# Float32 values in the first head group's attention, values' products set together, and squared blocks added before their product with ones

## The chip, the cores and the metric

The kernel runs on one core of a Trainium2 chip. The metric is the device time of one execution in microseconds (us); the runs shown of the kernel before took 2036.65, 2031.55 and 2031.51 us, with a median of 2031.55. The five engines are called TensorE (PE, with its weight loads as PEld), VectorE (DVE), ScalarE (ACT), GpSimd (POOL) and SyncE (SP).

## The reference

A bidirectional encoder of two layers on x of 1024 tokens by 1024, float32. Each layer mixes three groups of channels and then has a gated feed-forward part:

```python
h = _rmsnorm(x, g_pre_mix[l])
zf, zq, zk, zv, zm = jnp.split(h @ w_in[l], splits, axis=-1)     # 256, 512, 128, 128, 256
y_f = _fourier_mix(zf, w_fourier[l])
y_a = _window_attn(rope(q), rope(k), v, sink[l])    # 8 query heads, 2 key/value heads of 64
y_m = _memory_attn(zm, km, vm)                      # 4 heads over 256 memory rows
y = jnp.concatenate([_rmsnorm(y_f, ..), _rmsnorm(y_a, ..), _rmsnorm(y_m, ..)], -1) @ w_out[l]
x = x + _rmsnorm(y, g_post_mix[l])
gate, up = jnp.split(_rmsnorm(x, g_pre_ffn[l]) @ w_ffn_in[l], 2, axis=-1)
x = x + _rmsnorm((silu(gate) * up) @ w_ffn_out[l], g_post_ffn[l])
```

In the window attention a block of 128 queries sees its own block of keys and the one on each side (two at the ends). Query heads 0 to 3 share key/value head 0, and heads 4 to 7 share head 1; in the kernel these are head groups g = 0 and g = 1. The norms of y_f, y_a and y_m need the mean of squares of each token over its group's channels.

## The kernel before, in words

**Tiles.** Tokens are cut into NT = 8 tiles of 128. Most large products are made from numbers split into a high part, rounded to a format of TensorE (float32r), and the low rest: `split` (L174) copies the high part on ScalarE (L176) and subtracts on VectorE or POOL (L177). Such a product is three matmuls of high and low parts (`Acc`, L179). Some products are plain float32 matmuls, which the chip runs as two passes, so that the trace has two records for each.

**Stages of a layer.** Projections of keys, values and memory queries (`kvz`, L714), woven with the Fourier group; projections of queries (`q`, L761), woven with attention over memory (`mem_units`, L935); window attention of head group 0, woven with the output products of the Fourier and memory groups (`fm_units`, L1006) and the loads of w_out; window attention of group 1, woven with the output product of the attention group, the residual and the norm (`out`, L1061) and the first blocks of the feed-forward part (`Blocks`, L1081; `Quad`, L1135); then the feed-forward part, which the change does not edit.

**Window attention.** `att_scores` (L777) makes the scores of 4 heads, the exponentials (ScalarE, L801) and scales them by the reciprocal sums (POOL, L812). One tile later `att_values` (L817) transposes the probabilities of each key block j on TensorE into a PSUM tile `pT` (L825, four transposes), copies that to SBUF and multiplies it with the values. For group 0 the copy is a split (ScalarE L176, VectorE L177), and each of the two parts is the moving side (512 columns) of one matmul whose stationary side holds the high and the low values side by side (L840, tile `av`, 128 columns). `fold` (L855) then adds the two halves of the result: two copies on ScalarE (L861) and two additions on VectorE (L863). For group 1 `values_32` (L846) has first added high and low values into float32; the copy of `pT` is one ScalarE copy (L830) that separates heads by parity, and two float32 matmuls with 64 stationary columns, one for each half s of the array, multiply it (L833), just behind the copy of each block j.

**Attention over memory.** `mem_values` (L928) makes, for two heads, four float32 matmuls of 64 stationary and 512 moving columns (L932, tile `mav`): two memory blocks mt by two halves s.

**Sums of squares.** `group_scale` (L980) squares a tile on ScalarE (L985) into w blocks of 128 by 128, and adds over channels with w matmuls, each with a block as the stationary side and a 128x2 tile of ones as the moving side (L988, tile `ssp`). w is 2 for the memory group's tiles (from `fm_units`) and 4 for the attention tiles (from `out_prep`, L1050). The mean (L990, VectorE) and the power -1/2 (L992, POOL) give the scale by which the output product is later taken out of PSUM (L1031, L1072).

**Order.** The code issues work in units that `weave` and the loop at L1443 interleave; a scheduler in the framework then sets the order of each engine's instructions, and every engine works its own list in that order. Operands wait for each other by semaphores. Memory is laid out by hand: `at` gives places in a float32r and a float32 area in steps of 256 columns, and the places listed in `TURNED` are pieces of their own that `turned` and `reflex` turn from one type to the other; a piece is only turned when all that use it are done.

## Time and profile before

| what | value |
|---|---|
| three runs, us | 2036.65, 2031.55, 2031.51 (median 2031.55) |
| the profiled execution, us | 2032.38 |
| its span, first to last instruction, us | 2030.4 |
| granted TensorE clock over the span | 0.994 |
| instructions | 28325 |
| HBM | 220.11 MB read, 66.58 MB written, 141 GB/s |
| layer 0: group 0's wide value products | 223.1 to 281.5 us |
| layer 0: group 1's value products | 293.8 to 370.7 us |
| layer 1: the same two | 1218.6 to 1280.3 and 1288.7 to 1369.1 us |

The profile is one execution on the chip. Each engine's busy time is the union of its instructions; the chain of work that ended last follows, from the last instruction back, what released each step. Groups collect the instructions of a line. The matmuls of TensorE overlap in the pipeline, so the time that one holds the engine is read from its start to the next one's start and not from its own length.

### The profile page before, as it was taken

How to read it: one execution, taken by the hardware profiler on the slowest of the kernel's cores; microseconds unless marked ns; L12 is line 12 of the kernel's file. 1: busy time of each engine (PE TensorE's matmuls, PEld its weight loads, DVE VectorE, ACT ScalarE, POOL GpSimd, SP SyncE). 2: the span in 40 equal slices, each digit the busy share in tenths (PEclk: the TensorE clock that was granted, in tenths of full speed). 3: DMA queues.
4: the chain of work that ended last, by engine and by line, in shares of the span. 5: the costliest groups of instructions: out<-in, count | busy, mean ns of one | idle time of the engine just before them, and what ended most of it. 6: DMA issues, size and time to landing. Idle time of an engine off the chain costs nothing.

```text
span 2030.4 us, 28325 instructions
## 1 busy us (share of the span) xinstructions
PE 1984.7 (98%) x9587; PEld 1631.2 (80%) x9587; DVE 1492.6 (74%) x2346; ACT 1049.7 (52%) x2204; POOL 684.9 (34%) x811
## 2 busy tenths in 40 slices
PE   8999999999999999999999999999999999999998
PEld 7877878778888888887888778877788888887886
DVE  5566767897877776778876668679786776778766
ACT  6476877643333333554555768686333333346441
POOL 4344445224334333002423644451433433410011
PEclk9999999999999999999999999999999999999999
DMA  6110333434333324879831113244333323269973
GB/s 213 62 58 22 109 104 115 146 109 130 104 109 100 103 88 139 297 266 324 286 142 54 54 58 115 85 144 135 106 118 114 116 82 114 96 209 354 314 265 125
DMA packets 181889, 288.56 MB, mean 142 GB/s; under 512 B 15560, under 2 KB 81648, under 8 KB 181744
## 3 DMA queue, kind: packets, MB, share of 16 engines
q1 hardware_dynamic: 173680, 267.88, 39.7%
q10 hardware_dynamic: 8064, 18.88, 2.4%
q8 instruction: 75, 1.23, 0.2%
q14 instruction: 70, 0.57, 0.1%
HBM read 220.11 MB, written 66.58 MB: 141 GB/s over the span
## 4 chain that ended last, share of the span: by engine, by line
PE 86%; DVE 5%; DMA 3%; ACT 2%; issue 2%; POOL 1%; SPq 0%; DVEq 0%; POOLq 0%; ACTq 0%
PE fo L1330 17%; PE qc L1181 11%; PE qx L1181 11%; PE qy L1181 11%; PE mo L187 8%; PE qz L1181 5%; PE kvp L187 4%; PE qp L187 3%; PE zT L187 2%; PE sc L788 2%; PE pT L825 2%; PE av L833 1%; PE qa L1181 1%; PE mav L932 1%; PE av L840 1%
## 5 line engine op out<-in xcount | busy, mean ns | idle before, releaser
L1330 PE MATMUL fo<-arena_r 128*128 128x512 f32 x1512 | 354.2, 391 | 6.0 <-ACT big L1355 3.8
L1330 PEld LDWEIGHTS fo<-arena_r 128*128 128x128 f32 x1512 | 283.6, 188 | 65.6 <-ACT big L1355 4.6
L176 ACT CAST arena_r<-arena_f 128x512 fp32r<-128x512 f32 (+2 forms) x344 | 185.9, 571 | 179.5 <-DMA arena_f<-actd 66.6
L1181 PE MATMUL qc<-arena_r,flex 128*128 128x512 f32 x912 | 220.2, 390 | 0.0
L177 DVE TENSOR_TENSOR arena_r<-arena_f,arena_r 128x512 fp32r<-128x512 f32 x262 | 182.0, 727 | 46.9 <-ACT arena_r L176 39.0
L1171 ACT CAST flex<-arena_f 128x512 fp32r<-128x512 f32 x148 | 91.9, 621 | 235.0 <-PE qy L1181 73.3
L1181 PEld LDWEIGHTS qc<-arena_r,flex 128*128 128x128 f32 x912 | 171.2, 188 | 37.0
L1181 PE MATMUL qy<-arena_r,flex 128*128 128x512 f32 x576 | 139.9, 390 | 2.3 <-ACT flex L1171 2.3
L1171 ACT CAST arena_r<-arena_f 128x512 fp32r<-128x512 f32 x92 | 57.1, 621 | 159.1 <-DVE arena_f L1168 63.6
L1172 DVE TENSOR_TENSOR flex<-arena_f,flex 128x512 fp32r<-128x512 f32 x148 | 110.9, 750 | 28.4 <-ACT flex L1171 28.2
L1181 PEld LDWEIGHTS qy<-arena_r,flex 128*128 128x128 f32 x576 | 107.9, 188 | 25.3 <-ACT flex L1171 2.7
L1215 POOL TENSOR_TENSOR arena_f<-arena_f 128x512 f32<-128x512 f32 x36 | 47.3, 1315 | 237.5 <-ACT arena_f L1186 237.5
L1181 PE MATMUL qx<-arena_r 128*128 128x512 f32 x360 | 119.5, 389 | 0.0
L1181 PE MATMUL qy<-arena_r 128*128 128x512 f32 x480 | 116.7, 390 | 0.0
L1172 DVE TENSOR_TENSOR arena_r<-arena_f,arena_r 128x512 fp32r<-128x512 f32 x92 | 68.2, 742 | 63.2 <-ACT arena_r L1171 62.8
L1181 PE MATMUL qz<-arena_r,flex 128*128 128x512 f32 x320 | 106.8, 395 | 0.0
L1181 PEld LDWEIGHTS qy<-arena_r 128*128 128x128 f32 x480 | 90.3, 188 | 18.9 <-ACT arena_r L1171 0.2
L1168 DVE TENSOR_TENSOR arena_f<-arena_f 128x512 f32<-128x512 f32 x90 | 98.1, 1098 | 5.5 <-DMA arena_f<-in_w_ffn_in 3.9
L1222 POOL TENSOR_TENSOR arena_f<-arena_f 128x512 f32<-128x512 f32 x36 | 60.0, 1667 | 120.2 <-DVE arena_f L1221 120.2
L187 PE MATMUL mo<-big,arena_r 128*128 128x512 f32 x384 | 100.2, 399 | 0.3 <-ACT arena_f L1031 0.2
L1181 PE MATMUL qx<-flex,flex 128*128 128x512 f32 x304 | 100.1, 390 | 0.0
L1242 POOL TENSOR_TENSOR arena_f<-arena_f,flex 128x512 f32<-128x512 f32 x32 | 51.8, 1619 | 139.5 <-ACT flex L1233 83.7
(315 smaller groups left out, 4659.8 us busy)
## 6 DMA issues: line engine op xcount, KB each, us to landing
arena_f<-in_w_ffn_out SPq DMA_DIRECT2D x264, 256.0 KB, 4.7
actd<-arena_f SPq DMA_DIRECT2D x154, 256.0 KB, 2.5
arena_f<-actd SPq DMA_DIRECT2D x154, 256.0 KB, 4.4
arena_f<-in_w_ffn_in SPq DMA_DIRECT2D x46, 512.0 KB, 3.7
big<-in_w_ffn_in SPq DMA_DIRECT2D x40, 512.0 KB, 4.5
arena_f<-in_w_in SPq DMA_DIRECT2D x40, 256.0 KB, 2.9
arena_f<-in_x SPq DMA_DIRECT2D x16, 512.0 KB, 4.3
arena_f<-in_w_out SPq DMA_DIRECT2D x32, 256.0 KB, 2.7
```

The costliest lines, as they stand in the source:

```text
L176: nc.scalar.copy(hi, src)
L177: return (lo_eng or nc.vector).tensor_tensor(out=lo, in0=src, in1=f32(hi), op=ALU.subtract)
L187: mm(self.dst, a, b, start=self.i == 0, stop=self.i == self.n - 1)
L788: mm(pt, lhs, self.kst[g][i][:, k0 * P : k1 * P], start=i == 0, stop=i == 1)
L1168: nc.vector.tensor_tensor(out=s, in0=x, in1=y, op=op)
L1171: self.cast = nc.scalar.copy(w[:, 0], s)
L1172: nc.vector.tensor_tensor(out=w[:, 1], in0=s, in1=f32(w[:, 0]), op=ALU.subtract)
L1181: mm(pt, a, b, start=start and n == 0, stop=n == 11, skip_group_check=not start)
L1215: G(out=self.u2, in0=self.u2, in1=self.p1, op=ALU.add)
L1222: G(out=self.p5, in0=self.p1, in1=self.p5, op=ALU.add)
L1242: (G if i % 2 else V).tensor_tensor(out=a[i], in0=c, in1=g[i], op=ALU.mult)
L1330: mm(pt, ab[:, 0, x, sl], ab[:, 1, y], start=new and first and j == 0, stop=last and j == 2, skip_group_check=not new)
```

## The change

Three edits, and what goes with them:

- **Group 0 as group 1.** The values of both groups are kept in float32 (`v32`, one POOL copy for each tile in `kvz`), and group 0 takes the same path as group 1: one copy of `pT`, two 64-column float32 matmuls for each block, one eviction. In group 0 the copies of `pT` alternate between VectorE and ScalarE; in group 1 all are on ScalarE. The split of the values, `values_32` and `fold` are gone. There are 8 places for the copies in place of 4.
- **Products together.** In `att_values` the matmuls of a tile are issued after all its transposes and copies, with the last block first; in `mem_values` the four are issued with the second block and the second half first.
- **Squares added.** `group_scale` adds the squared blocks on VectorE by halving (4 to 2 to 1, or 2 to 1), so that one product with ones is left. Attention tiles 6 and 7 keep their four products.

Places 16 and 96 become pieces that can be turned; they are turned back to float32r in the pass i == NT of the loop, before the blocks of the feed-forward part that lie there.

```diff
-TURNED = {32: 8, 56: 8, 112: 8, 120: 4}
+TURNED = {16: 8, 32: 8, 56: 8, 96: 8, 112: 8, 120: 4}
...
+    def together(products):
+
+        for i, p_ in enumerate(products):
+            p_(i < 2, i >= len(products) - 2)
...
                 if half == 0:
+                    self.v32 = turned(96, 2, 2, NT, HD)[:, 0]
...
-            vst = self.vst[half][:, c]
-            split(vst[:, :, 0, :], vst[:, :, 1, :], r[:, P : 2 * P].rearrange("p (g d) -> p g d", g=2), nc.gpsimd)
+            nc.gpsimd.tensor_copy(self.v32[:, :, t, :], r[:, P : 2 * P].rearrange("p (g d) -> p g d", g=2))
...
             av = ps([512], "av", "av")
+            pfs = []
             for j in range(nk):
                 pT = ps([4, P], "pT", "pT")
                 for h in range(4):
                     nc.tensor.transpose(pT[:, h, :], es_[h // 2][:, h % 2, j * P : j * P + P], ident)
-                if g:
-
-                    pf = self.pfs[self.pfi % 4]
-                    self.pfi += 1
-                    nc.scalar.copy(pf, pT.rearrange("p (k s) q -> p s k q", s=2))
-                    for s in range(2):
-                        rhs = pf[:, s].rearrange("p k q -> p (k q)")
-                        mm(av[64 * s : 64 * s + 64, 0 : 2 * P], self.v32[:, k0 + j], rhs, start=j == 0, stop=j == nk - 1)
-                    continue
-                pp = phs(2, 512, dt=F32R)
-                ph, pl = pp[:, 0], pp[:, 1]
-                split(ph, pl, pT.rearrange("p h q -> p (h q)"))
-                lhs = self.vst[(k0 + j) // 4][:, (k0 + j) % 4, g].rearrange("p a d -> p (a d)")
-                for i, p_ in enumerate((ph, pl)):
-                    mm(av, lhs, p_, start=j == 0 and i == 0, stop=j == nk - 1 and i == 1)
-            if g:
-                nc.scalar.copy(dst, av[:, 0 : 2 * P].rearrange("p (k q) -> p k q", k=2))
-            else:
-                self.fold(av, dst)
+                pf = self.pfs[self.pfi % len(self.pfs)]
+                self.pfi += 1
+                (nc.vector.tensor_copy if self.pfi % 2 and not g else nc.scalar.copy)(pf, pT.rearrange("p (k s) q -> p s k q", s=2))
+                pfs.append(pf)
+            together([
+                lambda start, stop, j=j, s=s: mm(
+                    av[64 * s : 64 * s + 64, 0 : 2 * P], self.v32[:, g, k0 + j], pfs[j][:, s].rearrange("p k q -> p (k q)"),
+                    start=start, stop=stop,
+                )
+                for j in reversed(range(nk)) for s in range(2)
+            ])
+            nc.scalar.copy(dst, av[:, 0 : 2 * P].rearrange("p (k q) -> p k q", k=2))
+
+        def att_begin(self):
+
+            self.pfs, self.pfi = [p[:, i] for p in [turned(k, 4, 2, 2, P) for k in (112, 16)] for i in range(4)], 0
...
             av = ps([512], "mav", "av")
-            for mt in range(2):
-                for s in range(2):
-                    mm(av[64 * s : 64 * s + 64], self.mem.v[:, mt, 2 * pr + s], pfs[s][mt], start=mt == 0, stop=mt == 1)
+            together([
+                lambda start, stop, mt=mt, s=s: mm(av[64 * s : 64 * s + 64], self.mem.v[:, mt, 2 * pr + s], pfs[s][mt], start=start, stop=stop)
+                for mt in (1, 0) for s in (1, 0)
+            ])
...
-        def group_scale(self, parts, n, ring):
+        def group_scale(self, parts, n, ring, eng=None):
...
+            while eng and w > 1:
+                w //= 2
+                eng.tensor_tensor(out=sq[:, :w], in0=sq[:, :w], in1=sq[:, w : 2 * w], op=ALU.add)
...
-                st[t] = self.split_y((yf, ym), yys), self.group_scale((ym,), MW, sqs)
+                st[t] = self.split_y((yf, ym), yys), self.group_scale((ym,), MW, sqs, nc.vector)
...
-            self.prepped[t] = self.split_y(parts, yys), self.group_scale(parts, AW, sqs)
+            self.prepped[t] = self.split_y(parts, yys), self.group_scale(parts, AW, sqs, nc.vector if t < 6 else None)
...
+            if i == NT:
+                reflex(F32R, 16)
+                reflex(F32R, 96)
```

More of the change, by code (lines that the diff above doesn't have):

```diff
@@ L159, in tile_encoder @@
     zzs, dhs, tabs = run(112, 2, 4), run(64, 2, 4), run(72, 4, 2)
-    mps, phs, yys = Ring(56, 58, 32, 34), run(16, 3, 4), run(104, 2, 4)
+    mps, yys = Ring(56, 58, 32, 34), run(104, 2, 4)
     wcs, abs_ = Ring(112), Ring(80)
@@ L711, in kvz_load @@
             self.wkvz = load_w512(self.win, FW + AW, self.g)
-            self.vst, self.zst, self.kvr = {}, {}, {}
+            self.zst, self.kvr = {}, {}
         def kvz(self, t):
@@ L716, in kvz @@
             if c == 0:
-                self.vst[half] = at(96 + 4 * half, 4, 2, 2, HD, dt=F32R)
                 z = at(104 + 8 * half, 2, 2, 512, dt=F32R)
@@ L846, in values_32 @@
-        def values_32(self):
-            self.v32 = at(4, NT, HD)
-            for half in range(2):
-                v = self.vst[half][:, :, 1]
-                nc.gpsimd.tensor_tensor(out=self.v32[:, 4 * half : 4 * half + 4], in0=f32(v[:, :, 0]), in1=f32(v[:, :, 1]), op=ALU.add)
-            pf = turned(112, 4, 2, 2, P)
-            self.pfs, self.pfi = [pf[:, i] for i in range(4)], 0
-        def fold(self, av, dst):
-            cut = lambda ap: ap.rearrange("p (h s q) -> p s h q", s=2, q=P)
-            avh, avl = cut(av[0:64]), cut(av[64:128])
-            d = [dst[64 * s : 64 * s + 64] for s in range(2)]
-            for s in range(2):
-                nc.scalar.copy(d[s], avl[:, s])
-            for s in range(2):
-                nc.vector.tensor_tensor(out=d[s], in0=avh[:, s], in1=d[s], op=ALU.add)
+                pf = self.pfs[self.pfi % len(self.pfs)]
@@ L929, in mem_values @@
             av = ps([512], "mav", "av")
-            for mt in range(2):
-                for s in range(2):
-                    mm(av[64 * s : 64 * s + 64], self.mem.v[:, mt, 2 * pr + s], pfs[s][mt], start=mt == 0, stop=mt == 1)
+            together([
+                lambda start, stop, mt=mt, s=s: mm(av[64 * s : 64 * s + 64], self.mem.v[:, mt, 2 * pr + s], pfs[s][mt], start=start, stop=stop)
+                for mt in (1, 0) for s in (1, 0)
+            ])
             nc.vector.tensor_copy(self.ym[half][:, pr, :], av)
@@ L1429, in tile_encoder @@
         ld = mix.out_load()
+        mix.att_begin()
         weave(mix.att_units(0), fm[:2] + [u for i in range(4) for u in ld[2 * i : 2 * i + 2] + fm[2 + i : 3 + i]] + fm[6:])
```

1 line of the change is left out of this document (removed).

## The prediction

> **What bounds the kernel now.** I read the page first: busy time by engine, and then the chain of work that ended last.
>
> ```profile
> PE 1984.7 (98%) x9587; PEld 1631.2 (80%) x9587; DVE 1492.6 (74%) x2346; ACT 1049.7 (52%) x2204; POOL 684.9 (34%) x811
> ```
>
> ```profile
> PE 86%; DVE 5%; DMA 3%; ACT 2%; issue 2%; POOL 1%; SPq 0%; DVEq 0%; POOLq 0%; ACTq 0%
> ```
>
> Next I asked for busy time in four stretches of layer 0: the second half of the memory heads (172 to 210 us), the first head group's attention (210 to 286), the second group's attention with the output rows (286 to 372), and the handover to the feed-forward part (372 to 390). The columns are the stretch, its length, and busy us of each engine.
>
> ```profile
> 172.00:210.00 38.00, 37.20 (x203) 27.77 (x203) 24.07 (x45) 24.38 (x63) 15.83 (x27) 1.00 0.16 49
> 210.00:286.00 76.00, 74.32 (x399) 62.61 (x396) 57.75 (x176) 59.51 (x161) 33.82 (x55) 1.00 0.35 116
> 286.00:372.00 86.00, 85.71 (x511) 67.45 (x509) 56.35 (x125) 63.68 (x164) 44.48 (x77) 1.00 0.32 115
> 372.00:390.00 18.00, 15.94 (x72) 13.19 (x73) 17.18 (x25) 9.77 (x20) 5.22 (x10) 0.91 0.56 166
> ```
>
> In the first three, which are the ones that the change edits, TensorE is busy 98 to 99.7% and no other engine above 78%. There a microsecond less of TensorE work is a microsecond less of time, as long as no new wait takes its place. Only in the fourth is VectorE (17.18 of 18) the fuller one. So the sum is made on TensorE, from these four groups (busy us; both layers):
>
> ```profile
> L840 PE MATMUL av<-arena_r 128*128 128x512 f32 x88 | 31.0, 420 | 2.2 <-DVE flex L863 2.0 <-DVE arena_r L177 0.2
> L833 PE MATMUL av<-flex,arena_f 128*64 128x256 f32 x176 | 26.3, 398 | 0.0
> L988 PE MATMUL ssp<-const,arena_f 128*128 128x2 f32 x192 | 26.2, 240 | 1.1 <-DVE arena_r L438 1.1
> L932 PE MATMUL mav<-arena_f 128*64 128x512 f32 x64 | 23.4, 612 | 0.0
> ```
>
> A float32 matmul leaves two records: L833's 176 are 88 matmuls, L988's 192 are 96, L932's 64 are 32. The mean of one is the life of a pipelined instruction and no price; prices are start to start, from the timeline or the chain.
>
> **The change part by part. 1: the products with ones.** Two timeline pieces, of four and of eight records, each with the row that follows:
>
> ```profile
> 313.07 0.50 PE L988 MATMUL ssp<-const,arena_f 128*128 128x2 f32 x4
> 313.43 1.65 PE L187 MATMUL mo<-arena_r 128*128 128x512 f32 x6
> ```
>
> ```profile
> 1313.30 0.95 PE L988 MATMUL ssp<-const,arena_f 128*128 128x2 f32 x8
> 1314.11 0.53 PE L825 MATMUL pT<-const,arena_f 128*128 128x128 f32 x3
> ```
>
> Two products take 0.36 us and four take 0.81, so each further one is 0.45 / 2 = 0.225. Per layer the 8 Fourier/memory tiles go from 2 products to 1, and 6 of the 8 attention tiles from 4 to 1: 2 x (8 + 18) = 52 products fewer, **-11.7 us**.
>
> What is added for this is VectorE work. No row has a 128x256 or 128x128 float32 addition from two places of SBUF in this place; the nearest by shape are a 128x512 one and a 128x4 one:
>
> ```profile
> L355 DVE TENSOR_TENSOR arena_f<-arena_f,big 128x512 f32<-128x512 f32 x10 | 6.4, 686 | 0.0
> ...
> L807 DVE TENSOR_TENSOR den<-den,es 128x4 f32<-128x4 f32 x32 | 6.4, 201 | 12.1 <-ACT es L806 11.9
> ```
>
> Those bound each addition between 0.20 and 0.69 us; on the straight line between them 256 columns are 0.44 and 128 are 0.32, which I take. Twelve attention tiles with both and sixteen others with the short one make 12 x 0.76 + 16 x 0.32 = 14.2 us of VectorE, off the path: VectorE stands idle 18 of 76 and 30 of 86 us in those two stretches. Without that cover it would cost at most those 14.2 us. The latency also lies in the scale's chain (square, additions, product, scale), which is needed only when the tile's output product is evicted. In the built order VectorE's additions stand well ahead of that. VectorE before, in layer 0's second group, around the output rows (mo) of one tile:
>
> ```order
> L990 TENSOR_SCALAR ms_3674<-ssp_3669 128x1
> L805 TENSOR_TENSOR es_3837<-nmx_3830,const 128x4
> L1072 SCALAR_TENSOR_TENSOR arena_f<-mo_3847,grs_3676,arena_f 128x512
> L1072 SCALAR_TENSOR_TENSOR arena_f<-mo_3861,grs_3676,arena_f 128x512
> L321 SCALAR_TENSOR_TENSOR arena_f<-arena_f,nrs_3753 128x1024
> ```
>
> And VectorE now, at the same place (line numbers are the changed kernel's):
>
> ```order
> L1059 SCALAR_TENSOR_TENSOR arena_f<-mo_3660,grs_3490,arena_f 128x512
> L1059 SCALAR_TENSOR_TENSOR arena_f<-mo_3674,grs_3490,arena_f 128x512
> L972 TENSOR_TENSOR arena_f<-arena_f 128x256
> L972 TENSOR_TENSOR arena_f<-arena_f 128x128
> L321 SCALAR_TENSOR_TENSOR arena_f<-arena_f,nrs_3567 128x1024
> L364 SCALAR_TENSOR_TENSOR arena_f<-arena_f,rrs_3692 128x1024
> L977 TENSOR_SCALAR ms_3622<-ssp_3620 128x1
> ```
>
> The two additions have come in behind the evictions of the tile before; behind them on the queue waits the normalisation L321, 0.76 us later, for the transposes of a tile whose turn on TensorE is further on.
>
> **2: the memory heads' values.** Each matmul is 64 columns wide, and two of them, for the two halves of the array, run side by side. In the timeline of layer 1, one matmul alone, then three:
>
> ```profile
> 1193.81 0.60 PE L771 MATMUL qT<-const,arena_f 128*128 128x128 f32 x4
> 1194.34 1.07 PE L932 MATMUL mav<-arena_f 128*64 128x512 f32 x2
> 1195.35 0.50 PE L187 MATMUL mo<-big,arena_r 128*128 128x512 f32 x1
> 1195.68 0.64 PE L901 MATMUL ms<-flex,flex 128*128 128x256 f32 x4
> ...
> 1196.71 1.93 PE L932 MATMUL mav<-arena_f 128*64 128x512 f32 x6
> 1198.58 0.73 PE L187 MATMUL mo<-big,arena_r 128*128 128x512 f32 x2
> ```
>
> And all four of a call together, in layer 0:
>
> ```profile
> 198.50 1.94 PE L932 MATMUL mav<-arena_f 128*64 128x512 f32 x8
> 200.37 1.09 PE L922 MATMUL mpT<-const,arena_f 128*128 128x128 f32 x8
> ```
>
> Start to next start: one matmul 1.01 us, three 1.87, four 1.87. A matmul without its partner costs as much as the pair. Entering and leaving such a stretch costs too: the four transposes qT take 0.53, where twelve transposes in the chain go by at 1.31 / 12 = 0.109 each (below), so 0.09 more; leaving, the one matmul mo takes 0.33 where a 512-wide one takes 0.23 (part 3), 0.10 more at most, of which I take 0.06: 0.15 a stretch. The built order before and now, TensorE, at that place of layer 1:
>
> ```order
> L771 MATMUL qT_10337<-const,arena_f 128x128 x4
> L932 MATMUL mav_10370<-arena_f 64x512
> L187 MATMUL mo_10455<-big_10390,arena_r 128x512
> L901 MATMUL ms_10348<-flex_9790,flex_4070 128x256 x4
> L187 MATMUL mo_10455<-big_10390,arena_r 128x512 x2
> L932 MATMUL mav_10370<-arena_f 64x512 x3
> ```
>
> ```order
> L884 MATMUL ms_10299<-flex_9733,flex_4020 128x256 x4
> L187 MATMUL mo_10408<-big_10331,arena_r 128x512 x3
> L187 MATMUL mo_10408<-big_10332,arena_r 128x512 x3
> L914 MATMUL mav_10313<-arena_f 64x512 x4
> L187 MATMUL mo_10400<-big_10334,arena_r 128x512
> ```
>
> The lone first matmul (it was free while the other three still waited for a block) has gone to its partner. Counted over the order, the 32 matmuls stood in 17 stretches (nine of one, two of two, five of three, one of four) and now stand in 9 (two of two, seven of four): 9 x 1.01 + 2 x 1.01 + 6 x 1.87 = 22.3 against 2 x 1.01 + 7 x 1.87 = 15.1, and 8 stretches fewer at 0.15: **-8.4 us**.
>
> **3: the first group's values.** Rows of the chain: start, time it held the chain, what.
>
> ```profile
> 231.09 0.69 PE av L840 x3
> ...
> 293.89 0.58 PE av L833 x4
> ...
> 308.14 1.45 PE av L833 x12
> ...
> 316.22 1.31 PE pT L825 x12
> ```
>
> A 512-wide product of group 0 is 0.69 / 3 = 0.23. A pair of 64-column ones is 0.58, and in a longer stretch (1.45 - 0.58) / 2 = 0.435 for each further pair. Before: 88 wide products 20.2, and group 1's 44 pairs in 33 stretches 33 x 0.58 + 11 x 0.435 + 33 x 0.15 = 28.9; together 49.1. Now 88 pairs in 36 stretches: 36 x 0.58 + 52 x 0.435 + 36 x 0.15 = 48.9. **-0.2 us**: what group 0 loses by float32 values, standing together gives back in group 1. The order, TensorE, group 0 of layer 0, before and now:
>
> ```order
> L840 MATMUL av_2305<-arena_r 128x512 x3
> L988 MATMUL ssp_2410<-const,arena_f 128x2 x2
> L840 MATMUL av_2305<-arena_r 128x512 x2
> L825 MATMUL pT_2421<-const,arena_f 128x128 x4
> L187 MATMUL mo_2388<-big_2038,arena_r 128x512 x3
> L187 MATMUL mo_2388<-big_2039,arena_r 128x512 x3
> L840 MATMUL av_2305<-arena_r 128x512
> ```
>
> ```order
> L830 MATMUL pT_2419<-const,arena_f 128x128 x4
> L836 MATMUL av_2303<-flex_2093,flex_820 64x256 x2
> L836 MATMUL av_2303<-flex_2092,flex_820 64x256 x4
> L187 MATMUL mo_2380<-big_2039,arena_r 128x512 x3
> L187 MATMUL mo_2380<-big_2040,arena_r 128x512 x3
> L975 MATMUL ssp_2403<-const,arena_f 128x2
> ```
>
> Three pieces have become one of three pairs, and the transposes pT just ahead of it belong to the next tile.
>
> On the other engines this part only takes away. The relevant rows:
>
> ```profile
> L177 DVE TENSOR_TENSOR arena_r<-pT,arena_r 128x512 fp32r<-128x512 f32 x44 | 29.4, 687 | 1.3 <-ACT arena_r L176 0.8
> ...
> L863 DVE TENSOR_TENSOR flex<-av,flex 64x256 f32<-64x256 f32 x32 | 13.2, 413 | 1.0 <-ACT flex L861 0.7
> ...
> L933 DVE COPY arena_f<-mav 128x512 f32<-128x512 f32 x8 | 5.5, 692 | 4.7 <-PE mav L932 4.7
> ```
>
> VectorE loses the 44 low halves and the 32 folding additions (42.6 us) and gets 22 copies from PSUM, like L933's 0.69: 15.2. ScalarE keeps 22 of 44 copies. With the fold goes a wait of TensorE for it; next late there is one plain eviction on ScalarE:
>
> ```profile
> PE av L840 <- DVE flex L863: 2.0, 2, 1.3
> PE hTp L1106 <- DVE arena_f L321: 1.8, 1, 1.8
> ```
>
> **-2.0 us.** The second row, at the handover, I leave as it is: in the new order an output product stands ahead of those transposes, so it may go, but VectorE is full there. The summed values (L851) and the split of the values were on POOL and ScalarE beside a full TensorE: nothing.
>
> **New waits.** A stretch now starts with the block turned last. In the order I added up, at the prices above, what TensorE has between a tile's last transposes and its stretch: over 1.1 us in 31 of 32 tiles, mostly 3 to 9, against a copy of 0.6 to 0.7; in one tile 0.45. Between nothing and, say, one missed copy at every sixth stretch (8 x 0.65 = 5) I take +1.5.
>
> **Sum:** -11.7 - 8.4 - 0.2 - 2.0 + 1.5 = -20.8. The profiled execution took 2032.4 us with a span of 2030.4; the median of the three shown is 2031.55. So 2031.55 - 20.8 = **2010.8 us**.
>
> **The rivals.** (a) *The additions block GpSimd.* The two additions read SBUF twice, beside GpSimd's scaling of the probabilities, whose duration does vary:
>
> ```profile
> L812 POOL TENSOR_SCALAR arena_f<-arena_f,rden x128: 477/585/1017, 214.8 to 1358.1; 128x384 f32<-128x384 f32 x96, 128x256 f32<-128x256 f32 x32
> ```
>
> Its longest is 432 ns over its median, about one such addition. If every addition held a scaling up and TensorE waited behind it, 14.2 us come back: 2025.0. Against it: POOL is busy 34 of 76 and 44 of 86 us, and the median is 0.58. The Trainium skill, SBUF — State Buffer, on the shared port pair, says that a VectorE instruction with two SBUF inputs takes a port pair from GpSimd for its whole length; by that rule 14.2 us of POOL time go, though not of TensorE time. Chance 7%.
>
> (b) *TensorE waits at the head of each stretch: slower.* Were the 45 stretches to wait for the copy of the last block, nothing behind them could pass. From 20.8 / 45 = 0.46 us each the gain is gone; at a whole copy, 0.65 each instead of the 1.5 taken, it is -22.3 + 29.3 = +7.0: 2038.6. The cover counted above speaks against it. Chance 3%.
>
> (c) *Group 0's pairs do not run side by side*, like the lone mav: 44 x 0.435 = 19.1 more, 2029.9, no change. Group 1's, of the same shape, do. Chance 4%.
>
> **How the numbers follow.** Forecast 86%. Its own ends: no new wait and the 1.8 of the handover gone as well, with the 1.1 that products with ones waited (row L988), gives -25.2: 2006.3; with 5 us of new waits and 3 lost to the handover, -14.3: 2017.3. I widen that slightly toward (a): 2006 to 2018.5. A measurement of this kernel tells about 0.3% (6 us) from nothing; faster by more than that are the forecast and (a), 0.93, same (c), 0.04, slower (b), 0.03.
>
> **What would show it.** In the changed profile: 88 records with ones instead of 192; the memory values' busy time near 16 instead of 23.4; no lone 64-column matmul; stretches of 12 records at 1.45; TensorE at 98% or more from 210 us on, and layer 1 starting about 10 us earlier. It is wrong if waits of TensorE for the copies of pT or for POOL's scaling add up to more than 5 us.

## The result and the profile after

| | before | after |
|---|---|---|
| median of six runs each, in turn, us | 2032.17 (2031.51 to 2036.65) | 2020.88 (2016.27 to 2024.68) |
| ratio | | 0.994, 95% interval 0.9924 to 0.9955 |
| profiled execution, its span, us | 2032.38, 2030.4 | 2024.68, 2022.9 |

The kernel is 11.3 us faster, where 20.8 were forecast; the time lies above the range. The profiled execution after is the slowest of its six, 3.8 us over their median, and what is read from it has to be taken with that in mind.

**The work.** First the page's line of engines, after:

```profile
PE 1970.9 (97%) x9571; PEld 1616.1 (80%) x9571; DVE 1478.9 (73%) x2332; ACT 1026.5 (51%) x2150; POOL 687.5 (34%) x807
```

Then the groups of value products, memory values, additions and products with ones (busy us, mean ns; idle before them and its releaser):

```profile
L836 PE MATMUL av<-flex,flex 128*64 128x256 f32 x352 | 45.9, 389 | 0.5 <-DVE flex L833 0.4 <-ACT flex L833 0.2
L914 PE MATMUL mav<-arena_f 128*64 128x512 f32 x64 | 16.3, 626 | 0.6 <-ACT arena_f L907 0.6
L972 DVE TENSOR_TENSOR arena_f<-arena_f 128x128 f32<-128x128 f32 (+1 forms) x40 | 15.8, 398 | 5.7 <-ACT arena_f L969 5.5
L975 PE MATMUL ssp<-const,arena_f 128*128 128x2 f32 x88 | 13.4, 235 | 0.6 <-DVE arena_f L972 0.5
```

The work is as the prediction asked for: 88 records with ones, memory values at 16.3, additions at 15.8 us (14.2 taken), and TensorE waits only 0.5 us for the copies of pT. Added up from each start to the next, the three groups of products went from 22.15 to 9.50, from 22.21 to 15.68 and from 47.06 to 43.43 us: 22.8 less.

**The stretches.** Busy times in the prediction's four stages; first layer 0 after (memory heads, group 0, group 1, handover). Its third and fourth rows do not compare one by one with the prediction's: there the layer's last 24 output products stood in the fourth stretch (375.5 to 382 us), and here the third ends behind the last of them.

```profile
169.00:206.00 37.00, 35.90 (x205) 28.18 (x205) 24.92 (x47) 26.09 (x66) 16.94 (x27) 1.00 0.16 50
206.00:281.00 75.00, 74.16 (x426) 56.85 (x423) 46.48 (x149) 48.35 (x134) 33.01 (x53) 1.00 0.35 118
281.00:371.00 90.00, 88.56 (x518) 71.40 (x517) 68.71 (x150) 69.73 (x180) 49.64 (x80) 1.00 0.38 126
371.00:389.00 18.00, 15.72 (x66) 12.62 (x65) 15.63 (x25) 9.76 (x18) 3.88 (x7) 0.91 0.43 132
```

Group 1's attention in layer 1, before:

```profile
1293.00:1377.00 84.00, 84.00 (x498) 66.17 (x497) 61.42 (x121) 62.86 (x157) 43.88 (x71) 1.00 0.40 131
```

and after:

```profile
1288.00:1369.00 81.00, 79.34 (x461) 63.16 (x460) 59.77 (x130) 62.90 (x157) 44.12 (x70) 1.00 0.38 128
```

In that last stretch TensorE worked 84.00 of 84.00 us before, and 79.34 of 81 after: 4.7 us less work, 3.0 us less time (eight transposes for the feed-forward part, some 0.9 us at 0.11 each, stand in it before and not after). In layer 0 the last output product of the stage starts 11.0 us earlier (370.8 instead of 381.8), and the 100th product of the feed-forward part only 6.0.

**Where it went.** No single wait took it. The largest rows of TensorE's waits after, from group 1 of layer 0 into the feed-forward part:

```profile
PE qa L1168 <- ACT flex L1158: 2.3, 1, 2.3
PE qz L1168 <- DVE arena_r L1159: 1.9, 1, 1.9
PE mo L187 <- DVE arena_f L1059: 1.1, 2, 0.9
```

and in layer 1, from the query projections to the handover:

```profile
PE yfT L618 <- ACT flex L611: 2.0, 2, 1.8
PE mpT L905 <- POOL arena_f L895: 1.6, 3, 0.9
PE qc L1168 <- ACT arena_f L1173: 1.3, 1, 1.3
PE pT L830 <- POOL arena_f L816: 0.9, 2, 0.5
PE qp L187 <- POOL big L177: 0.7, 2, 0.4
```

Before, the four largest rows of the same two views were these:

```profile
PE hTp L1106 <- DVE arena_f L321: 1.8, 1, 1.8
PE qx L1181 <- DVE flex L1172: 1.0, 1, 1.0
PE qp L187 <- DVE big L407: 1.7, 1, 1.7
PE av L840 <- DVE flex L863: 0.7, 1, 0.7
```

The rows after name three engines and as many lines as rows. Some of them cost more than they last. Busy times in four consecutive windows of 3.41 us around the wait for qa (2.3 us in which TensorE stands still, up to 376.2), with the granted clock behind POOL's column:

```profile
369.41:372.82 3.41, 3.41 (x16) 2.81 (x15) 3.41 (x6) 2.05 (x4) 0.19 (x1) 1.00 1.17 299
372.83:376.24 3.41, 1.13 (x6) 0.60 (x4) 3.41 (x7) 1.57 (x4) 1.48 (x2) 1.00 0.86 281
376.24:379.65 3.41, 3.41 (x8) 2.73 (x9) 3.41 (x6) 1.92 (x4) 0.29 (x1) 0.50 0.05 16
379.65:383.06 3.41, 3.41 (x20) 2.87 (x20) 2.17 (x4) 1.63 (x4) 1.18 (x2) 1.00 0.01 2
```

A window with 1.13 us of work is followed by one at half clock, in which TensorE counts as busy and does 8 matmuls where the next does 20: 1.7 us more for the wait.

So a span divides into three parts, counted from the first key/value product: **waits** (each start to the next one's start, less the price of that kind of instruction, 0.11 us for a transpose or a record with ones and 0.23 for 512 columns, where over 250 ns is left), **half clock** (half the time at a granted clock of 0.50, as far as the last matmul), and **work**, the rest. Before: 1928.0 work, 28.3 waits, 6.8 half clock. After: 1907.0, 37.0 and 11.9. The work fell by 21.0, waits took 8.7 back and the clock 5.1; the -7.5 between the two profiled spans is these and 0.3 before the first product.

### The profile page after: what moved, and what is told of

Read it like the earlier page. It is cut to its first block, busy times and chain, and to the rows that moved or that the text cites. A ratio compares the mean times of both kernels' runs of the same rounds, so it can differ in the third digit from the quotient of the medians.

```text
span 2022.9 us, 28165 instructions
## 1 busy us (share of the span) xinstructions
PE 1970.9 (97%) x9571; PEld 1616.1 (80%) x9571; DVE 1478.9 (73%) x2332; ACT 1026.5 (51%) x2150; POOL 687.5 (34%) x807
## 4 chain that ended last, share of the span: by engine, by line
PE 64%; DVE 5%; DMA 3%; issue 2%; POOL 2%; ACT 2%; SPq 0%; DVEq 0%; POOLq 0%; ACTq 0%
PE fo L1317 14%; PE qc L1168 10%; PE qx L1168 10%; PE qy L1168 10%; PE qz L1168 5%; PE mo L187 3%; PE kvp L187 2%; PE qp L187 2%; DMA arena_f<-actd 1%; PE zT L187 1%; DMA arena_f<-in_w_ffn_out 1%; PE av L836 1%; PE sc L792 1%; DVE arena_r L177 1%; PE pT L830 1%
## 5 line engine op out<-in xcount | busy, mean ns | idle before, releaser
L1317 PE MATMUL fo<-arena_r 128*128 128x512 f32 x1236 | 296.5, 391 | 3.6 <-ACT big L1342 3.1
L1317 PEld LDWEIGHTS fo<-arena_r 128*128 128x128 f32 x1236 | 232.4, 189 | 53.1 <-ACT big L1342 4.0
L176 ACT CAST arena_r<-arena_f 128x512 fp32r<-128x512 f32 (+1 forms) x286 | 155.6, 572 | 145.8 <-DMA arena_f<-actd 44.2
L1158 ACT CAST flex<-arena_f 128x512 fp32r<-128x512 f32 x148 | 91.9, 621 | 229.3 <-PE qy L1168 66.8
L177 DVE TENSOR_TENSOR arena_r<-arena_f,arena_r 128x512 fp32r<-128x512 f32 x214 | 147.1, 716 | 28.8 <-ACT arena_r L176 26.8
L1317 PE MATMUL fo<-flex 128*128 128x512 f32 x612 | 153.8, 394 | 3.3 <-ACT arena_r L176 3.3
L1158 ACT CAST arena_r<-arena_f 128x512 fp32r<-128x512 f32 x92 | 57.1, 621 | 162.5 <-DVE arena_f L1155 67.3
L1317 PEld LDWEIGHTS fo<-flex 128*128 128x128 f32 x612 | 115.7, 190 | 27.5 <-issue 3.4
L1168 PE MATMUL qy<-arena_r,flex 128*128 128x512 f32 x544 | 133.8, 389 | 0.0
L1159 DVE TENSOR_TENSOR flex<-arena_f,flex 128x512 fp32r<-128x512 f32 x148 | 110.9, 750 | 28.8 <-ACT flex L1158 28.7
L1168 PE MATMUL qx<-flex,arena_r 128*128 128x512 f32 x384 | 125.7, 389 | 0.0
L1159 DVE TENSOR_TENSOR arena_r<-arena_f,arena_r 128x512 fp32r<-128x512 f32 x92 | 68.2, 741 | 63.1 <-ACT arena_r L1158 62.8
L177 DVE TENSOR_TENSOR flex<-arena_f,flex 128x512 fp32r<-128x512 f32 x110 | 82.2, 768 | 43.1 <-ACT flex L176 37.2
L1168 PE MATMUL qy<-flex,arena_r 128*128 128x512 f32 x320 | 105.0, 389 | 0.0
```

The source lines that it names most:

```text
L176: nc.scalar.copy(hi, src)
L177: return (lo_eng or nc.vector).tensor_tensor(out=lo, in0=src, in1=f32(hi), op=ALU.subtract)
L1158: self.cast = nc.scalar.copy(w[:, 0], s)
L1159: nc.vector.tensor_tensor(out=w[:, 1], in0=s, in1=f32(w[:, 0]), op=ALU.subtract)
L1168: mm(pt, a, b, start=start and n == 0, stop=n == 11, skip_group_check=not start)
L1317: mm(pt, ab[:, 0, x, sl], ab[:, 1, y], start=new and first and j == 0, stop=last and j == 2, skip_group_check=not new)
```

## The experiments

The theories, as the expectations name them. **A**: the handover to the feed-forward part is bound by VectorE, and what TensorE saves ahead of it is lost there (**A'**: as much, GpSimd being no help to it). **B**: the additions, with two operands in SBUF, hold up GpSimd and VectorE's own queue. **C**, later **L**: the framework's scheduler finds another order for each kernel, and the order decides which waits come up. **S**: the parts add up. **R** and **W** stand where they come in. Each was timed beside the kernel before on the same chip; ratios are to that, and differences in us are of medians. The kernel before came to 2032.2 to 2033.6 us on the chips used, so a difference between two kernels timed on different chips can be off by 1.4 us. The three parts are of the one profiled execution, which can lie well off its kernel's median: 7.8 us over it for mem_only, 5.4 for squares_fm, 4.4 for values_only, 3.8 for the changed kernel, and 4.2 under it for ones_again. The work differs by 3.5 us at most between the orders of one kernel; single waits have to be taken with that in mind.

| kernel | median us | ratio (95%) | work | waits | half clock |
|---|---|---|---|---|---|
| mem_only | 2024.65 | 0.9957 (0.9941 to 0.9973) | 1918.6 | 34.7 | 11.9 |
| squares_only | 2037.22 | 1.002 (1.0008 to 1.0032) | 1913.4 | 40.9 | 11.9 |
| values_only | 2035.45 | 1.0013 (1.0001 to 1.0025) | 1927.3 | 33.2 | 10.2 |
| blocks_pool | 2026.71 | 0.9969 (0.9958 to 0.998) | 1907.7 | 37.9 | 11.9 |
| no_squares | 2030.52 | 0.9996 (0.9984 to 1.0008) | 1920.5 | 34.9 | 8.5 |
| squares_fm | 2028.76 | 0.9975 (0.9962 to 0.9988) | 1914.4 | 42.2 | 11.9 |
| flip_copies | 2023.20 | 0.9951 (0.9935 to 0.9966) | 1909.1 | 35.6 | 5.1 |
| adds_twice | 2035.14 | 1.0009 (0.9997 to 1.002) | 1906.2 | 43.2 | 17.1 |
| blocks_act | 2020.95 | 0.995 (0.9933 to 0.9968) | 1908.1 | 34.6 | 10.2 |
| after_first | 2024.04 | 0.9965 (0.9952 to 0.9978) | 1909.6 | 36.7 | 8.5 |
| squares_first | 2025.69 | 0.9965 (0.9951 to 0.998) | 1916.9 | 34.3 | 6.8 |
| mem_squares | 2018.76 | 0.9941 (0.9925 to 0.9956) | 1905.9 | 37.3 | 5.1 |
| before_fm | 2032.86 | 0.9999 (0.9987 to 1.0011) | 1927.8 | 28.8 | 8.5 |
| before_att | 2035.20 | 1.0006 (0.9992 to 1.002) | 1929.4 | 30.7 | 6.8 |
| before_first | 2036.46 | 1.0021 (1.0009 to 1.0032) | 1930.2 | 32.2 | 5.1 |
| mem_squares_first | 2028.04 | 0.9977 (0.9964 to 0.999) | 1905.5 | 43.7 | 10.2 |
| ones_again | 2033.59 | 1.0002 (0.9989 to 1.0014) | 1916.9 | 32.9 | 11.9 |
| after_att | 2025.41 | 0.996 (0.9945 to 0.9975) | 1907.1 | 39.6 | 10.2 |

### The parts by themselves

**mem_only**, on the kernel before:

```diff
-            for mt in range(2):
-                for s in range(2):
-                    mm(av[64 * s : 64 * s + 64], ..., start=mt == 0, stop=mt == 1)
+            together([... for mt in (1, 0) for s in (1, 0)])
```

> The kernel before, with one of the four parts only: the memory heads' four products of a tile stand together. Start to next start, these products took 6.5 us less in the changed kernel. Theory A (TensorE's saved time reaches the end unless VectorE is the bound at the handover to the FFN, where what is saved ahead of it is given back): about half is left, -3 to -4 us against before. Theory B (the additions of squared blocks lock GpSimd out of SBUF and its scaling of probabilities comes late): no additions here, so the whole -6.5 stays. Theory C (each extra wait of TensorE costs its clock as well, by chance): -6.5 with single runs up to 4 us apart, the slower ones at the lower mean granted clock.

-7.65 us: the whole of it came out, as B and C said; A has lost half of it and is wrong here. The prediction had -8.4. The waits in the table are those of the slowest of its five runs.

**squares_only**, on the kernel before: the additions in `group_scale` and its two calls, as in the change.

> The kernel before, with one part only: squared blocks are added on VectorE, for 88 products with ones in place of 192. Start to next start, these products took 12.65 us less in the changed kernel. A (VectorE is the bound at the handover): the additions stand ahead of the handover and also fill VectorE, -5 to -7 us against before. B (GpSimd locked out by the additions): 21 scalings lengthened by some 0.3 us each, of which TensorE waits for a part, -6 to -9 us, and the long scalings of the changed kernel (over 640 ns) are all here, with TensorE rows that name GpSimd's scaling as the releaser. If neither holds: -12.

None was right: 4.9 us *slower*, with 14.6 us less work. The largest loss is one place of layer 0. VectorE there:

```profile
330.72 1.75 DVE L364 SCALAR_TENSOR_TENSOR arena_f<-arena_f,rrs 128x1024 f32<-128x1024 f32 x1 [1.41 <-POOL rrs L237]
332.39 0.83 DVE L988 TENSOR_TENSOR arena_f<-arena_f 128x128 f32<-128x128 f32 x1
333.14 0.54 DVE L789 CUSTOM_DVE_ANT_0 arena_f<-sc,const 128x384 f32<-128x384 f32 x1
...
333.62 1.21 DVE L365 TENSOR_TENSOR arena_f<-arena_f 128x1024 f32<-128x1024 f32 x1
334.76 0.68 DVE L177 TENSOR_TENSOR arena_r<-big,arena_r 128x512 fp32r<-128x512 f32 x1
335.36 0.55 DVE L789 CUSTOM_DVE_ANT_0 arena_f<-sc,const 128x384 f32<-128x384 f32 x1
```

and TensorE's waits from 280 to 385 us:

```profile
PE av L833 <- DVE rmax L789: 2.2, 1, 2.2
PE mo L187 <- POOL arena_r L177: 1.8, 1, 1.8
PE sc L788 <- DVE rmax L789: 1.1, 1, 1.1
```

The row maxima (L789) stand behind a normalisation, an addition (L988, here 0.83 us beside a subtraction of GpSimd's that takes 1.73) and two more long instructions. VectorE works its list in order, so the row maxima come late, and TensorE waits for them 2.2 and 1.1 us; two windows at half clock follow.

**values_only**, on the changed kernel: the memory values and both calls of `group_scale` as before.

> The changed kernel without the additions and with the memory heads' products in the old order: what is left is the first head group's float32 values, its stretches, its copies on two engines and the storage. The prediction has -2.2 us for it (-0.2 of products, -2.0 of folds no longer waited for); start to next start the products took 3.6 us less. A (handover): 0 to -2 against before. B (GpSimd locked out by additions): -2 to -4, since there are none. C (a new order of the program and turned storage that let blocks 5 and 6 of the FFN's input wait for tile 7's values): this part alone costs, so 0 to +5, with the waits of the handover (for the FFN's first weights and blocks) in it.

+3.2, within C's bounds and outside A's and B's. Its work is 1927.3, 0.7 less than before (-0.2 was forecast), its waits 4.9 more, though it takes 24.7 us off VectorE (1467.9 busy against 1492.6). Its profiled execution is the second slowest of twelve.

**blocks_pool**, on the changed kernel:

```diff
-            self.lo = split(hi, lo, s)
+            self.lo = split(hi, lo, s, nc.gpsimd if i in (5, 6) else None)
```

> The changed kernel, with the low halves of FFN input blocks 5 and 6 made on GpSimd and not on VectorE: some 5.5 us of VectorE's work per layer leave the stretch at the handover in which it is busy without a gap. A (VectorE is the bound at the handover): 3 to 5 us under the changed kernel (about 2017), with TensorE's waits at the first FFN products (2.4 us for the block's weights, 2.05 us for a later weight) gone or halved in both layers. B (GpSimd locked out by additions) and C (chance of order and clock): the same as the changed kernel within 2 us, the waits moved rather than gone.

5.8 us over the changed kernel's median, so no theory's number. What VectorE was spared at the handover of layer 0 it lost beside GpSimd: from the last output product to the 100th of the feed-forward part 31.9 us passed, against 30.3 in the changed kernel. The two engines at the handover of this kernel, VectorE first:

```profile
369.16 1.78 DVE L1159 TENSOR_TENSOR flex<-arena_f,flex 128x512 fp32r<-128x512 f32 x1
...
373.80 0.67 DVE L1159 TENSOR_TENSOR arena_r<-arena_f,arena_r 128x512 fp32r<-128x512 f32 x1
...
374.47 1.69 DVE L1159 TENSOR_TENSOR arena_r<-flex,arena_r 128x512 fp32r<-128x512 f32 x1
```

```profile
368.66 1.74 POOL L177 TENSOR_TENSOR arena_r<-flex,flex 128x512 fp32r<-128x512 f32 x1
...
374.14 1.47 POOL L177 TENSOR_TENSOR arena_r<-flex,flex 128x512 fp32r<-128x512 f32 x1
```

The same subtraction takes VectorE 0.67 us where it starts first (GpSimd's begins 0.34 us later), and 1.7 to 1.8 where one of GpSimd's is under way. The Trainium skill (SBUF — State Buffer, "SBUF: two separate sides") has an exclusive lock, held for a whole instruction, between GpSimd and a VectorE operation with two SBUF inputs, and the one that starts second blocks. By that rule VectorE is the loser here, and the rows agree: both long subtractions end 0.54 to 0.55 us behind GpSimd's.

### With and without the additions, and another order

**no_squares**: the changed kernel with both calls of `group_scale` as before.

> The changed kernel without the additions of squares (192 products with ones again); the other parts stay. Theory S (the parts' own measured times add up): memory heads together -7.65 us and group 0's values +3.15 in the runs of the single parts give -4.5 against before, some 2028, that is 7 us over the changed kernel. Theory B (the additions cost more on VectorE and GpSimd than the 12.65 us of products that they remove, as the single part's +4.9 says, by delaying row maxima and scalings that TensorE waits for): the changed kernel without them is faster than with them, 2016 or less, -16 against before. Theory L (which waits come up is set by the order that the framework's scheduler finds anew for each kernel, not by a part): anywhere between -4 and -14.

2030.5: in the changed kernel the additions *earn* 9.6 us, of the 11.7 forecast. B falls as the cause of the shortfall. The rows of GpSimd's scaling, without the additions:

```profile
L816 POOL TENSOR_SCALAR arena_f<-arena_f,rden 128x384 f32<-128x384 f32 (+1 forms) x128 | 77.4, 625 | 63.0 <-DVE rden L813 28.7 <-ACT arena_f L1018 9.7 <-DVE ms L977 5.1
```

and with them, in the changed kernel:

```profile
L816 POOL TENSOR_SCALAR arena_f<-arena_f,rden 128x384 f32<-128x384 f32 (+1 forms) x128 | 74.9, 604 | 57.4 <-DVE rden L813 31.5 <-ACT flex L833 11.2 <-ACT arena_f L1018 5.1
```

The long scalings (over 640 ns, of the 192 of both kinds of attention: 3 before, 21 after) are 22 here, with no addition in the kernel, so the additions are not what brings them.

**squares_fm**: the changed kernel, `self.group_scale(parts, AW, sqs)` in `out_prep`.

> The changed kernel with additions for the Fourier/memory group's 16 tiles only; the 12 attention tiles keep four products (24 additions fewer, 36 products with ones more, 8.1 us by the price of one). S: 8.1 over the changed kernel, 2029. B: the attention tiles' additions stand beside VectorE's row maxima, evictions and normalisations, so taking them away gives back more than it costs: 2015 to 2020. L: 2018 to 2029, with TensorE's waits in other places than in the changed kernel.

2028.8, as S had it: the attention tiles' additions are worth 7.9 of 8.1 us.

**flip_copies**, on the changed kernel:

```diff
-(nc.vector.tensor_copy if self.pfi % 2 and not g else nc.scalar.copy)(pf, ...)
+(nc.vector.tensor_copy if not self.pfi % 2 and not g else nc.scalar.copy)(pf, ...)
```

> The changed kernel, with the copies of the transposed probabilities of group 0 given to the other engine of the two each: same work on every engine within one copy, in an order that the scheduler finds anew. S and B: within 1 us of the changed kernel's 2020.9. L: some us away from it on either side, with TensorE's waits (37 us over 250 ns each from the first projection on in the changed kernel) different by the same amount, plus 1.7 us for each half-clock stretch more or less.

2.3 us slower, but the intervals overlap. Its profiled execution, the fastest of its six, is 4.9 us shorter than the changed kernel's, the slowest of its six, with 6.8 us less at half clock.

**adds_twice**, on the changed kernel, behind the addition:

```diff
+                eng.tensor_tensor(out=sq[:, w : 2 * w], in0=sq[:, w : 2 * w], in1=sq[:, w : 2 * w], op=ALU.add)
```

> The changed kernel with a second addition of the same size behind each one, on the half of the squares that is no longer read: 40 additions more, 15 us of VectorE's time at the first ones' lengths, no work for TensorE. S (VectorE's work lies beside TensorE's): within 1 us. B: what the additions cost is paid again; if they ate the single part's whole gain, 12.65 + 4.9 = 17.5 us for 40 additions, then up to +17 over the changed kernel, and at the least +6; more scalings over 640 ns than the 21 of the changed kernel. L: +-4 with no relation to the number of long scalings.

14.3 us slower, for 40 more additions of together 16.9 us on VectorE, and with 23 long scalings instead of 21. S fails; the price is B's, but the long scalings hardly became more. The largest wait of the stretch of group 1 in layer 1 is for a normalisation in VectorE's queue:

```profile
PE hTp L1094 <- DVE arena_f L321: 3.9, 1, 3.9
PE mo L187 <- DVE arena_f L1060: 1.1, 2, 0.9
```

VectorE, at 73% over the span, had room for one such set of additions and none for a second, in this one order; what orders alone can do is seen below.

### The handover, and the same instructions in another order

**blocks_act**, on the changed kernel; the low halves of blocks 5 and 6 hold the copy, not the difference:

```diff
-            self.lo = split(hi, lo, s)
+            if i in (5, 6):
+                nc.scalar.copy(hi, s)
+                self.lo = nc.scalar.copy(lo, s)
+            else:
+                self.lo = split(hi, lo, s)
```

> The changed kernel, with the low halves of FFN input blocks 5 and 6 made by a copy on ScalarE (which leaves out their subtraction, so the low halves hold other numbers): the same 5.5 us of VectorE's work per layer leave the handover as in the run with GpSimd, but no second engine with two operands in SBUF comes beside VectorE. In that run VectorE's own weight subtractions went from 0.68 to 1.7 us where one of GpSimd's ran beside them. Theory A' (the handover is bound by VectorE's work, and handing it to GpSimd gave nothing because the two slow each other): 3 to 6 us under the changed kernel, 2015 to 2018, the stage from the last output row to the 100th gate product (qz) 3 to 4 us shorter in each layer. If the handover is a chain of latencies and VectorE's load does not matter: within 2 us. Theory L (orders): some us on either side, with the waits in other stages.

0.995 against the changed kernel's 0.994: nothing gained in time, so A' is not borne out by the median. The traces show more. From the last output product to the 100th of the feed-forward part, layer 0 took 25.4 us before, 30.3 in the changed kernel and 26.1 here, and layer 1 27.1, 30.2 and 29.8. So in layer 0 VectorE's load did hold the handover, as far as one execution tells (the changed kernel's other orders took 27.5 to 30.7). By the 100th qz 2.3 and 0.8 us were left, where A' had 3 to 4; and this execution, 5.7 us ahead of the changed kernel's at the last group of products (fo), lost 2.8 of that there.

**after_first**, on the changed kernel, and **squares_first**, on squares_only, both with the two calls exchanged:

```diff
-                st[t] = self.split_y((yf, ym), yys), self.group_scale((ym,), MW, sqs, nc.vector)
+                gs = self.group_scale((ym,), MW, sqs, nc.vector)
+                st[t] = self.split_y((yf, ym), yys), gs
...
-            self.prepped[t] = self.split_y(parts, yys), self.group_scale(parts, AW, sqs, nc.vector if t < 6 else None)
+            gs = self.group_scale(parts, AW, sqs, nc.vector if t < 6 else None)
+            self.prepped[t] = self.split_y(parts, yys), gs
```

> The changed kernel with the squares issued ahead of the split of the same tile in place of behind it, for the Fourier/memory and the attention tiles: the same instructions on every engine, and only the scheduler's order differs. Theory S or B: 2020.9 within 1 us. L: several us off (the copies given to the other engine came to 2023.2), work of TensorE the same 1907 us, waits and half-clock time not.

> The kernel before with the additions of squares alone (2037.2), with the same exchange of squares and split: the same instructions on every engine. B (additions alone cost 17.5 us of waits because VectorE is fuller with the first group's splits and folds): 2037 within 2 us. L (it was that order's luck): 2025 to 2035, with the 3.6 us wait for row maxima in layer 0 or the 3.7 us wait for the FFN's weight in layer 1 gone.

3.2 us slower the one (5.1 by the ratios), where the intervals just overlap and the waits are much the same (36.7 against 37.0): no evidence for any theory. 11.5 us *faster* the other, which is L's, and clear of the intervals. In squares_first the wait for row maxima is gone. TensorE's waits from 280 to 385 us, to be set beside those of squares_only:

```profile
PE qa L1186 <- ACT flex L1176: 2.2, 1, 2.2
PE pT L825 <- POOL arena_f L812: 1.2, 3, 0.8
PE mo L187 <- POOL arena_r L177: 0.2, 1, 0.2
```

**mem_squares**, on the kernel before: mem_only's and squares_only's edits together.

> The kernel before with the memory heads' products together and the additions, without group 0's float32 values. S with the single parts' measured times: -7.65 + 4.9 = -2.8, 2029.5. B (the additions pay only when group 0's values leave VectorE 27 us freer): 2028 to 2032. L (the additions' loss in the single run was that order): towards -7.65 - 9.6 = -17 (the 9.6 is what they earn in the changed kernel), that is 2015 to 2026, and then group 0's float32 values are what costs in the changed kernel.

2018.8, in L's range. It is level with the changed kernel (0.9941 and 0.994), so group 0's float32 values show no gain there; -2.2 was forecast for them. No variant beat the changed kernel by more than the measurement tells.

### Is it the order of the kernel before, or TensorE's lead?

**R**: the kernel before has a lucky order that any change loses. **W**: waits grow because TensorE has less to do. The next three are the kernel before with the exchange in `fm_units` alone, in `out_prep` alone, and in both; the fourth is mem_squares with both.

> The kernel before, with the squares issued ahead of the split in the Fourier/memory tiles only: the same instructions on every engine, another order. Theory R (the order of the kernel before is one in which few waits come up, and any new order of the same work has more: 28 us of them before against 34 to 43 in every other kernel so far): 2036 to 2044. Theory W (waits grow because TensorE's work shrinks, whatever the order; orders only scatter): 2032 on average over the three exchanges, some higher and some lower by up to 6.

> The kernel before, with the squares issued ahead of the split in the attention tiles only: the same instructions on every engine, another order in the second head group's attention and behind it. R: 2036 to 2044. W: 2032 on average over the three exchanges, some higher and some lower by up to 6.

> The kernel before, with both exchanges at once. R: 2036 to 2044. W: 2032 on average over the three exchanges, some higher and some lower by up to 6. By W the three should scatter around the kernel before, by R none should be under it.

> The kernel with the memory heads' products together and the additions (2018.8), with both exchanges: the same instructions, another order. Theory L: up to 6 us either side of 2018.8. If the exchange itself is a better place for the squares (it gave -11.5 with the additions alone, +3.2 in the changed kernel): 2008 to 2016.

Neither as it was put. None of the three is measurably faster than the kernel before (+0.6, +2.9, +4.2 us), and only the last is measurably slower; on average that is 2.6 us, and too little for R. The fourth lost 9.3 us by its order alone (7.3 by the ratios), more than the 6 that L had.

**ones_again**, on the changed kernel:

```diff
             for i in range(w):
                 mm(pss, sq[:, i], ones, start=i == 0, stop=i == w - 1)
+            for i in range(2 * len(parts) - w):
+                mm(pss, sq[:, 0], ones, start=True, stop=True)
```

> The changed kernel with the one product with ones that is left made again on TensorE, once in the Fourier/memory tiles and three times in the 12 attention tiles: 52 products, 11.7 us of TensorE's work at the price of 0.225, and nothing more on the other engines. Theory W (with less work TensorE runs into the other engines' chains, so that part of what it saves comes back as waits; the three orders of the kernel before have 28 to 32 us of waits, the three of the changed kernel 36 to 37): work that is put back takes waits away, +5 to +8 against the changed kernel, about 2027, waits near 33. If the waits belong to the edits (additions, copies, storage) and not to TensorE's lead: +11 to +13, some 2033, waits 36 to 37 as before. Orders add up to 4 us either way.

> The changed kernel with the squares issued ahead of the split in the attention tiles only, a fourth order of the same instructions. L: 2018 to 2027, work 1907 to 1910, waits 35 to 37.

By its time (+12.7) the first speaks against W: all of the 11.7 us put back is paid. By its profiled execution (+4.8 us to the changed kernel's, waits 32.9) it speaks for W, but that execution is the second fastest of its 12, and the changed kernel's the slowest of its 6. The medians weigh more, but orders scatter by as much, so the question stays open. after_att is a fourth order of the changed kernel, 4.5 us over the first, which the intervals do not separate; its waits, 39.6, lie above L's 35 to 37.

**What the four orders of each say.** The kernel before and its three exchanges, and the changed kernel with flip_copies, after_first and after_att:

| mean of four | ratio | work | waits | half clock |
|---|---|---|---|---|
| before | 1.0007 | 1928.9 | 30.0 (28.3 to 32.2) | 6.8 |
| changed | 0.9954 | 1908.2 | 37.2 (35.6 to 39.6) | 8.9 |

The work is 18 to 23 us less whichever two are compared, 20.7 on average; the waits are 7.2 more, without overlap, and half clock 2.1, with overlap (5.1 to 8.5 and 5.1 to 11.9): -11.4 together, and the ratios say -10.7. The profiled executions of the two sets lie on average 0.4 us over and 0.2 under their medians. Counted between the same products of the program, the added waits lie mostly at the handover of layer 0, from the last output product to the 100th of the feed-forward part (from 0.9 to 3.6), in group 1 of layer 1 (from 0.2 to 2.8) and in group 0 of layer 1 (from 2.5 to 3.5); group 1 of layer 0 has 2.9 and 2.3.

## Why the prediction was wrong, by its own steps

- **Products with ones, -11.7: right as work, and nearly right as time** in the changed kernel (12.65 start to next start; 9.6 by leaving them out). By themselves the same additions cost 4.9 in one order and gave 7.9 in another.
- **Memory values, -8.4: right** (-7.65 alone; 6.5 start to next start, where the sum for these rows had 7.2 and 1.2 more around them).
- **Group 0's values, -0.2: right as work** (-0.7 in values_only; -3.6 start to next start in the changed kernel), wrong as time: +3.2 alone, and nothing in the changed kernel against mem_squares.
- **"There a microsecond less of TensorE work is a microsecond less of time, as long as no new wait takes its place"** and the two terms that filled this in, folds' waits -2.0 and **new waits +1.5**: this step failed. The folds' waits went (2.0 us in row L840 before), but the net of -0.5 came to +8.7 in the profiled pair and +7.2 over the orders. The cover was counted for one kind of wait only, the copies of pT, and for that one it held (0.5 us). Even the prediction's own sign of failure, over 5 us of waits for these copies or for POOL's scaling, did not show: 0.5 and 3.0. Most of the waits that came are for lines that the change does not touch: weight casts and subtractions (L1158, L1159), the Fourier group's copies (L611), evictions (L1059), GpSimd's scalings (L895, L816).
- **The clock was left out.** In the profiled pair it is 5.1 us of the difference, in the averages 2.1, which is within what the orders scatter by. It is also part of what single runs scatter by: over the 181 timed runs of the experiments, 0.001 less mean granted clock goes with 1.0 us more (correlation 0.59).
- **Rival (a)** came nearest in time by another cause: long scalings did go from 3 to 21, but they do so without any addition. **(b)** falls: 0.5 us. **(c)** falls: pairs run side by side; all 20 stretches of 12 records take 1.45 us, as forecast.
- **The handover** was left as it was, with a doubt about VectorE. In the profiled execution it gave back 5 us of layer 0, the largest single piece. With VectorE's load taken away there, 4.2 us of that came back in one execution and nothing in the median, so the doubt was about the right place, and does not explain the shortfall by itself. The prediction's stretches also ended 10 us short of the layer's last output product.
- **The signs.** TensorE at 98% held in layer 0's attention (74.16 of 75, 88.56 of 90) and just about in layer 1's (79.34 of 81, where it had been 84.00 of 84.00), so this sign told little. Layer 1 starts 3.1 us earlier, not 10.

What stays open is why these waits come. The parts can be set against it by their medians: what a kernel's work fell by, less what its time fell by, is 1.8 us for mem_only, 3.9 for values_only, 5.8 for no_squares, which has both, and 9.7 for the changed kernel (8.8 to 13.2 over its four orders). Of the 6.4 and 4.9 us of waits that the table adds for mem_only and values_only, 4.1 and 4.8 lie between the feed-forward part's output products of layer 0 and the start of layer 1, which no edit touches, in executions that are among the slowest of theirs. For ones_again the same difference is 11.5, although 9.9 us of work are put back: that points at the edits and their orders more than at TensorE's lead, but no run separates the two.

## What to carry to other kernels

In this kernel, with TensorE at 98% and a scheduler that orders the engines, work taken from it came out by about half: count the sum of work, then expect new waits in places that the edit does not touch, and put a term on them. Before a part is judged, time it in two or three orders of the same instructions (exchange two independent statements): here that moved a kernel by up to 11.5 us, as much as the whole change. An engine at 73% with a strict queue may have room for the first 15 us of extra work and none for the second.

## What the runs showed of the hardware

**A wait of 2 us can halve the clock.** The clock events lie on a fixed grid of 3.41 us. Over all 20 profiled executions, from the first key/value product on and outside of stretches already at half clock, a window with TensorE busy under 40% was followed by half clock 55 times of 55; from 40 to 45% 22 of 23; 45 to 50% 13 of 26; 50 to 55% 7 of 17; 55 to 70% 3 of 93; above that never (11069 windows). Half clock lasts one or two windows, 1.7 us lost in each. The same wait may cost it or not, by where the grid falls: after's wait of 1.9 us for qz, up to 438.7 us, did not. The Trainium skill (TensorE: Matmul & The Clock Gate, "What's actually happening") has the free-running window of about 3.4 us and the half rate, and the grid agrees; it puts the fall behind an idle window, and "HAM oscillation — how this bites in real kernels" warns of idle gaps over 3.4 us. Here windows that were busy for 45 to 50%, with 1.7 to 1.9 us of waits in them, were enough 13 times of 26.

**Two engines with two operands in SBUF slow each other both ways**: in blocks_pool VectorE's subtraction of 128x512 went from 0.67 to 1.78 us, and GpSimd's of the same shape from 1.28, the shortest of the eight from the same tiles, to 1.74.
